# An output projection as one pipeline of 16 token tiles in three stages, with the first up product among its last tiles

## The chip, the cores and the metric

The kernel runs on one core of one Trainium2 chip. The metric is the device time of one execution in microseconds (us); the number given for a kernel is the median of its runs.

## What is computed

One block of a diffusion model on 2048 tokens of 1024 channels. A mixing part makes a vector y of 1024 channels for every token (four branches, not touched here). Then, as the reference has it:

```
mix   = y @ w_out
h     = x + mod2 * rmsnorm(mix, g_post_mix)
hl    = rmsnorm(h, g_pre_ffn) * (1 + mod4) + mod3
f     = conv_ffn(hl, ffn_w_up, ffn_conv_w, ffn_conv_b, ffn_w_down, 32 rows)
out   = h + mod5 * rmsnorm(f, g_post_ffn)
```

conv_ffn multiplies hl by w_up (1024 x 5632), runs a 3x3 convolution over the tokens as a grid of 32 rows of 64, multiplies gelu of one half by the other half, and multiplies by w_down (2816 x 1024).

## The kernel before, in words

Every matrix product is made of three f16 products (high times high, high times low, low times high), with power-of-two scales found on the chip. Tokens are handled in four chunks of 512; a chunk has four tiles of 128 tokens. The kernel is written against a tile framework: each engine's instruction order is settled when the program is built, by program order as the priority and by buffers coming free, and the framework sets the semaphores. A tile with a tag has so many buffers (bufs); the next tile of that tag waits for the oldest to be read out. Memory comes from pools that are opened and closed like a stack; a pool opened on the place of a closed one waits for the closed one's tiles.

**Mixer.** It leaves y in two places: 512 channels in on-chip tiles Y[0] to Y[3] (one per chunk, 8 KB of each partition), the others in DRAM tiles ybc[n].

**Output projection** (lines 833 to 891). The loop runs over the chunks 3, 0, 1, 2. For each chunk it first makes the chunk's scale (lines 834 to 839): a reduction, a tiny product with ones in a PSUM bank of tag C (line 122, the tile "sct"), and some one-column VectorE operations. Then for each of its four tiles:

- Projection. SyncE's queue loads x's rows (xr, line 846, two buffers) and y's DRAM half (yr, line 850, three buffers). VectorE splits y in high and low f16 halves (split, lines 309 and 310, four instructions, tile ysp, three buffers). TensorE runs 48 matmuls of 512 columns into two PSUM banks of tag A, of four (lines 859 to 863).
- Residual (lines 864 to 880). ScalarE squares the two banks with a sum (867), GpSimd takes a power of -1/2 (160), VectorE scales the banks (873), GpSimd adds xr (875), the rows are stored to hlat in DRAM (876), ScalarE squares and sums again (878), GpSimd takes another power (160), VectorE scales into xr (880).
- Channels (lines 881 to 891). TensorE transposes the eight 128x128 blocks into two banks of tag C, of two (885), ScalarE applies scale and shift (888), VectorE makes the high half of hT (890), GpSimd the low half (891). hT, all tokens with channels on the partitions, is what the up products read.

The weights of up product 0 are loaded and split (load_up, lines 812 to 828) ahead of the last chunk, n == 2.

**Feed-forward** (lines 898 to 1076). PSUM's pool ps0 (banks A 4, B 2, C 2) is closed and ps1 (V two of two banks, B 2, C 2) opened; the pool ff is opened on the memory of Y and w_out. 22 products: up(c) (lines 926 to 934) writes z of 128 x 2 x 32 x 64 in eight steps of 24 matmuls (lines 356 to 358) with one eviction each (932); z has two buffers. One loop turn c issues up(c), the weights of up(c + 1) (which take a statistic, whose product with ones is line 122 again, in a bank B of ps1 now; a ScalarE copy 822, another 824, and a GpSimd subtraction 825), the convolution of z of c - 1 on VectorE (lines 938 to 967, 32 instructions of line 956 and two of line 964), and the down products of earlier pairs.

Of the kernel before, what the change touches and what calls it, by code (L numbers as in the profile page):

```python
# [7 lines left out]
F32 = mybir.dt.float32  # L8
F16 = mybir.dt.float16
BF16 = mybir.dt.bfloat16  # L10
I32 = mybir.dt.int32
AF = mybir.ActivationFunctionType
OP = mybir.AluOpType
AX = mybir.AxisListType

D = 1024
L = 2048
LC = 256
CH = 512
NCH = L // CH  # L20
# [48 lines left out]
def block_kernel(ctx: ExitStack, tc: tile.TileContext, x, xT, ctx_d, ctxT, cc, crow, cols_d, wm01, bm01, wmT,  # L69
                 win, wuv, gw, pw, wsT, gnorm, wout, wup, wdn, ident_d, out):  # L70
    nc = tc.nc
    V, A, G, T, S = nc.vector, nc.scalar, nc.gpsimd, nc.tensor, nc.sync
# [4 lines left out]
    small = ctx.enter_context(tc.tile_pool(name="small", bufs=4))  # L77
# [14 lines left out]
    def pA(name):  # L92
        return bank("A", name)

    def pB(name):
        return bank("B", name)

    def pC(name):
        return bank("C", name)
# [3 lines left out]
    hlat = dram.tile([L, D], F32, name="hlat")  # L103
# [52 lines left out]
    def rsqrt(dst, src, n, scale):  # L156

        t = small.tile([128, 12], F32, tag="rst", name="rst")
        V.tensor_scalar(t[:, :n], src, scale, EPS, op0=OP.mult, op1=OP.add)
        G.tensor_tensor(dst, t[:, :n], mhalf[:, :n], op=OP.pow)  # L160

    hT = const.tile([128, 2, KT, L], F16, name="hT")

    wmix = tc.tile_pool(name="ymix", bufs=1)
    ymix = wmix.__enter__()
    Y = [ymix.tile([128, 4, CH], F32, name=f"Y{n}") for n in range(NCH)]
    wsp = tc.tile_pool(name="wsp", bufs=8)
    wspp = wsp.__enter__()
    mixc = tc.tile_pool(name="mix", bufs=1)
# [138 lines left out]
    def split(slot_hi, slot_lo, raw, sc, after=()):  # L308
        hold(V.tensor_scalar(slot_hi, raw, sc[:, 0:1], None, op0=OP.mult), after)
        V.scalar_tensor_tensor(slot_lo, raw, sc[:, 0:1], slot_hi, op0=OP.mult, op1=OP.subtract)  # L310
# [42 lines left out]
    def mm3(ps, wh, wl, hh, hl):  # L353

        for k in range(KT):
            T.matmul(ps, wh(k), hh(k), start=(k == 0), stop=False)  # L356
            T.matmul(ps, wh(k), hl(k), start=False, stop=False)  # L357
            T.matmul(ps, wl(k), hh(k), start=False, stop=(k == KT - 1))  # L358
# [10 lines left out]
    for j in range(4):  # L369
        r = win_raw[j]  # L370
# [308 lines left out]
    wo = {}  # L679
# [150 lines left out]
    gm2 = row_of("gm2", on_, 0, col("gqm", 0, 8))  # L830
    gs_f, sc_f, _ = fold("gsf", col("gpf", 0, 8), mcol[:, 0, 8:16], mcol[:, 0, 16:24])

    for n in (3, 0, 1, 2):
        ysc = small.tile([128, 2], F32, tag="ysc", bufs=2, name="ysc")
        yt = small.tile([128, 1], F32, tag="yt", bufs=2, name="yt")
        V.tensor_reduce(yt, ysq[:, n, :], axis=AX.X, op=OP.add)
        scales(ysc, yt)
        oinv = small.tile([128, 1], F32, tag="oinv", bufs=2, name="oinv")
        V.tensor_scalar(oinv, ysc[:, 1:2], wosc[:, 1:2], None, op0=OP.mult)
        if n == 2:  # L840
            wn, lu = load_up(0)
            list(lu)
        for tt in range(4):
            tok = n * CH + tt * 128
            xr = on_.tile([128, D], F32, tag="xr", name="xr")
            S.dma_start(xr, x[tok:tok + 128, :])
            ysp = op_.tile([128, 2, 8, 128], F16, tag="ysp", bufs=3, name="ysp")
            tw = slice(tt * 128, (tt + 1) * 128)
            yr = op_.tile([128, 4, 128], F32, tag="yr", bufs=3, name="yr")
            S.dma_start(yr, ybc[n][:, :, tw])  # L850
            split(ysp[:, 0, 4:8], ysp[:, 1, 4:8], yr, ysc)
            split(ysp[:, 0, 0:4], ysp[:, 1, 0:4], Y[n][:, :, tw], ysc)
            ps = [pA(f"wo{h}") for h in range(2)]
            order = (6, 7, 4, 5, 0, 1, 2, 3)
            for i, k in enumerate(order):
                wk = wo[k]
                st, sp = i == 0, i == 7
                for h in range(2):
                    T.matmul(ps[h], ysp[:, 0, k, :], wk[:, 0, h * CH:(h + 1) * CH], start=st, stop=False)  # L859
                for h in range(2):  # L860
                    T.matmul(ps[h], ysp[:, 0, k, :], wk[:, 1, h * CH:(h + 1) * CH], start=False, stop=False)  # L861
                for h in range(2):
                    T.matmul(ps[h], ysp[:, 1, k, :], wk[:, 0, h * CH:(h + 1) * CH], start=False, stop=sp)  # L863
            hl = on_.tile([128, D], F32, tag="hl", bufs=2, name="hl")
            ms = small.tile([128, 2], F32, tag="ms", name="ms")
            for h in range(2):
                A.activation(hl[:, h * CH:(h + 1) * CH], ps[h], AF.Square, scale=oinv, accum_out=ms[:, h:h + 1])
            m1 = small.tile([128, 2], F32, tag="m1", name="m1")
            V.tensor_tensor(m1[:, 0:1], ms[:, 0:1], ms[:, 1:2], op=OP.add)
            rsqrt(m1[:, 1:2], m1[:, 0:1], 1, 1.0 / D)  # L870
            V.tensor_scalar(m1[:, 0:1], m1[:, 1:2], oinv, None, op0=OP.mult)
            for h in range(2):
                V.scalar_tensor_tensor(hl[:, h * CH:(h + 1) * CH], ps[h], m1[:, 0:1], gm2[:, h * CH:(h + 1) * CH],
                                       op0=OP.mult, op1=OP.mult)
            G.tensor_tensor(hl, hl, xr, op=OP.add)
            S.dma_start(hlat[tok:tok + 128, :], hl)
            m2 = small.tile([128, 2], F32, tag="m2", name="m2")
            A.activation(xr, hl, AF.Square, accum_out=m2[:, 0:1])
            rsqrt(m2[:, 1:2], m2[:, 0:1], 1, 1.0 / D)
            V.tensor_scalar(xr, hl, m2[:, 1:2], None, op0=OP.mult)  # L880
            h32 = on_.tile([128, 8, 128], F32, tag="h32", bufs=1, name="h32")
            for h in range(2):
                pt = pC("tr")
                for k in range(4):
                    T.transpose(pt[:, k * 128:(k + 1) * 128], xr[:, (4 * h + k) * 128:(4 * h + k + 1) * 128], ident)
                for k in range(4):
                    kk = 4 * h + k
                    A.activation(h32[:, kk, :], pt[:, k * 128:(k + 1) * 128], AF.Identity,  # L888
                                 bias=gs_f[:, 1, kk:kk + 1], scale=gs_f[:, 0, kk:kk + 1])
            V.tensor_scalar(hT[:, 0, :, tok:tok + 128], h32, 1.0, None, op0=OP.mult)  # L890
            G.tensor_tensor(hT[:, 1, :, tok:tok + 128], h32, hT[:, 0, :, tok:tok + 128], op=OP.subtract)

    oc.__exit__(None, None, None)
    wsp.__exit__(None, None, None)
# [1 line left out]


    banks["ffn"] = True
    ff = ctx.enter_context(tc.tile_pool(name="ff", bufs=2))
    oc2.__exit__(None, None, None)  # L900
    fa = ctx.enter_context(tc.tile_pool(name="fa", bufs=2, side="right"))
    close_psum()
    open_psum("ps1", 0, 2, 2)
# [4 lines left out]
    def load_down(gi):  # L908
# [11 lines left out]
        for r, w in zip(rs, ws):  # L920
# [1 line left out]
            A.activation(r, r, AF.Copy, scale=dnsc[:, gi, 0:1])  # L922
            G.tensor_tensor(w[:, 1, :], r, w[:, 0, :], op=OP.subtract)  # L923
            yield

    def up(c, z, w):
        for b in range(4):
            for ab in range(2):
                ps = pB("up")
                mm3(ps, lambda k: w[:, 0, ab, k, :], lambda k: w[:, 1, ab, k, :],  # L930
                    lambda k: hT[:, 0, k, b * CH:(b + 1) * CH], lambda k: hT[:, 1, k, b * CH:(b + 1) * CH])
                A.activation(z[:, ab, b * 8:(b + 1) * 8, :], ps.rearrange("p (r x) -> p r x", x=64),  # L932
                             AF.Identity, scale=upinv[:, c:c + 1])
                yield

    TAPS = [(dy, dx) for dy in (-1, 0, 1) for dx in (-1, 0, 1) if (dy, dx) != (0, 0)]

# [99 lines left out]
    for c in range(NP + 1):  # L1037
        gi, i = divmod(c, GRP)
        if c < NP:
            z = ff.tile([128, 2, 32, 64], F32, tag="z", name="z")  # L1040
            upn, lu = up(c, z, wn), nothing
            if c + 1 < NP:
                wn, lu = load_up(c + 1)
            if i == 0:
                ld = load_down(gi)
        else:
            upn = lu = nothing
        for s in range(8):
            next(upn, None)
            if s > 0:  # L1050
                next(lu, None)
                if s % 2 == 0:
                    next(ld, None)
            if c != NP - 1:
                for _ in range(1 if c < NP else 2):
                    if next(dn, queue) is queue and queue:
                        dn = queue.pop(0)
                        next(dn)
            next(cvn, None)
            if s % 4 == 3 and c > 0 and i == 0:  # L1060
                q = s // 4
                queue.append(down(gi - 1, q, *split_g(gi - 1, q, gs, gsq)))
        if 2 <= c < 10:
            next(mf)
        if c == 10:
            next(mf, None)
            gm5 = row_of("gm5", fa, 3, col("gqf", 0, 8))
        if c < NP:
            if i == 0:
                gs = [[], []]  # L1070
                gsq = small.tile([128, 2, GRP], F32, tag="gsq", bufs=2, name="gsq")
            cvn = conv(c, z, gs, [gsq[:, q, i:i + 1] for q in range(2)])
# [97 lines left out]
```

## Time and profile before

| | |
|---|---|
| median of 3 runs | 2252.57 us (2251.51 to 2254.48) |
| the profiled execution | 2258.45 us, its span 2256.7 us |
| TensorE busy | 2055.7 us, 91% of the span |
| VectorE busy | 1602.1 us, 71% |
| ScalarE busy | 1195.1 us, 53% |
| GpSimd busy | 600.4 us, 27% |
| mean granted clock of TensorE | 0.95 |

The span is the profiled execution from its first instruction to its last, and all stretches below are counted from the span's start. PE is TensorE's matmuls, PEld its weight loads, DVE VectorE, ACT ScalarE, POOL GpSimd, SP SyncE. A matmul's end is modelled, so neighbours overlap in the rows; the distance of two starts is the time that one takes. The granted clock is 1.00 for 2.4 GHz and 0.50 for 1.2 GHz.

### The profile page before, as it was taken

What the parts mean: (1) busy time and instruction counts of PE and PEld (TensorE: products, weight loads), DVE (VectorE), ACT (ScalarE), POOL (GpSimd) and SP (SyncE); (2) the same over time, 40 slices, a digit from 0 to 9 for tenths busy, and PEclk for the clock granted to TensorE, in tenths of its full rate; (3) what the DMA queues carried; (4) which work ended last, traced back from release to release, by engine and by line L of the source; (5) the groups of instructions that cost most, each with busy time, mean ns of one, the idle gap of its engine ahead of it and who ended that gap; (6) DMA issues with size and microseconds to landing.
All of it is one profiled execution on the core that took longest, in us unless ns stands there. A gap on an engine that the chain in (4) does not pass through costs nothing.

```text
span 2256.7 us, 24365 instructions
## 1 busy us (share of the span) xinstructions
PE 2055.7 (91%) x9215; PEld 943.1 (42%) x9215; DVE 1602.1 (71%) x2218; ACT 1195.1 (53%) x1661; POOL 600.4 (27%) x453
## 2 busy tenths in 40 slices
PE   6878989797788779999999999999999999999964
PEld 1533444343334334444444444444444444444421
DVE  6687778999343449977778677867677776777844
ACT  4666755453433355655565554656555564646421
POOL 2332333543333430101122121212121121112144
PEclk8889999898888889999999999999999999999987
DMA  7521143413222221223546454545545454454387
GB/s 284 203 87 51 64 153 122 135 45 125 97 80 80 79 71 37 94 85 123 96 76 130 86 103 88 107 81 100 90 88 108 85 102 72 97 94 84 58 231 252
DMA packets 77514, 239.48 MB, mean 106 GB/s; under 512 B 7890, under 2 KB 18514, under 8 KB 72530
## 3 DMA queue, kind: packets, MB, share of 16 engines
q1 hardware_dynamic: 56660, 162.42, 21.4%
q0 software_dynamic: 20736, 75.51, 20.4%
q8 instruction: 72, 1.18, 0.2%
q14 instruction: 46, 0.38, 0.1%
HBM read 128.84 MB, written 109.05 MB: 105 GB/s over the span
## 4 chain that ended last, share of the span: by engine, by line
PE 57%; issue 4%; DMA 3%; DVE 3%; POOL 2%; ACT 1%; POOLq 0%; SPq 0%; DVEq 0%; ACTq 0%
PE up L356 12%; PE up L357 12%; PE up L358 12%; PE dn L1003 6%; PE dn L1005 6%; PE dn L1004 6%; DVE cv L956 1%; DMA ac<-accd 1%; PE wo L863 1%; PE wo L861 1%; PE wo L859 1%; DMA out_dram<-hr 1%; DMA hr<-hlat 1%; ACT h L888 1%; POOL hr L1027 1%
## 5 line engine op out<-in xcount | busy, mean ns | idle before, releaser
L956 DVE SCALAR_TENSOR_TENSOR cv<-z,cols,cv 128x1008 f32<-128x1008 f32 (+2 forms) x704 | 874.6, 1251 | 290.9 <-ACT cv L949 196.4
L356 PE MATMUL up<-hT,uw 128*128 128x512 f16 x1408 | 534.3, 379 | 4.3 <-ACT h L888 2.2
L357 PE MATMUL up<-hT,uw 128*128 128x512 f16 x1408 | 534.3, 379 | 0.0
L358 PE MATMUL up<-hT,uw 128*128 128x512 f16 x1408 | 534.1, 379 | 0.0
L1018 POOL DMA_DIRECT2D accd<-dd x144 | 124.6, 865 | 763.0 <-ACT dd L1014 756.8
L932 ACT ACTIVATE z<-up,upinv 128x512 f32<-128x512 f32 x176 | 120.8, 686 | 350.8 <-PE up L358 350.2
L1003 PE MATMUL dn<-dw,gs 128*128 128x512 f16 x704 | 271.4, 386 | 35.7 <-DVE ac L1009 32.1
L1014 ACT ACTIVATE dd<-dn,gdi 128x512 f32<-128x512 f32 x320 | 214.2, 681 | 114.0 <-PE dn L1005 107.9
L1004 PE MATMUL dn<-dw,gs 128*128 128x512 f16 x704 | 271.4, 385 | 0.0
L1005 PE MATMUL dn<-dw,gs 128*128 128x512 f16 x704 | 269.4, 385 | 0.0
L357 PEld LDWEIGHTS <-uw 128*128 128x128 f16 x1408 | 137.8, 98 | 169.2 <-issue 5.0
L356 PEld LDWEIGHTS <-uw 128*128 128x128 f16 x1408 | 139.0, 99 | 165.2 <-issue 0.8
L358 PEld LDWEIGHTS <-uw 128*128 128x128 f16 x1408 | 137.9, 98 | 166.6 <-issue 0.8
L825 POOL TENSOR_TENSOR uw<-ur,uw 128x2048 f16<-128x2048 f32 x22 | 89.5, 4068 | 201.2 <-ACT ur L824 201.2
L136 ACT ACT_TABLE_LOAD x77 | 98.8, 1283 | 48.2 <-PE rp L440 29.9
L1004 PEld LDWEIGHTS <-gs 128*128 128x128 f16 x704 | 69.6, 99 | 119.5 <-issue 44.8
L949 ACT ACTIVATE cv<-z,cols 128x1024 f32<-128x1024 f32 x88 | 106.1, 1205 | 2.3
L1003 PEld LDWEIGHTS <-gs 128*128 128x128 f16 x704 | 73.0, 104 | 81.2 <-issue 5.1
L1005 PEld LDWEIGHTS <-gs 128*128 128x128 f16 x704 | 69.8, 99 | 86.2 <-issue 5.5
L859 PE MATMUL wo<-wo,ysp 128*128 128x512 f16 x256 | 81.3, 401 | 10.0 <-ACT gm L804 7.8
L863 PE MATMUL wo<-wo,ysp 128*128 128x512 f16 x256 | 77.4, 387 | 4.9 <-DVE ysp L310 4.9
L923 POOL TENSOR_TENSOR dw<-dr,dw 128x1024 f16<-128x1024 f32 x22 | 46.4, 2124 | 129.8 <-PE dn L1005 100.6
(299 smaller groups left out, 3042.8 us busy)
## 6 DMA issues: line engine op xcount, KB each, us to landing
accd<-dd POOLq DMA_DIRECT2D x144, 512.0 KB, 5.4
ur<-in_wup_dram SPq DMA_DIRECT2D x22, 1024.0 KB, 5.6
wm<-in_wmT_dram SPq DMA_DIRECT2D x64, 256.0 KB, 2.9
dr<-in_wdn_dram SPq DMA_DIRECT2D x22, 512.0 KB, 4.1
hT<-in_wm_dram SPq DMA_DIRECT2D x8, 1024.0 KB, 14.6
xt<-in_xT_dram SPq DMA_DIRECT2D x8, 1024.0 KB, 7.3
ro<-in_wout_dram SPq DMA_DIRECT2D x16, 512.0 KB, 3.6
xr<-in_x_dram SPq DMA_DIRECT2D x16, 512.0 KB, 4.1
```

Of the source, the lines that this page charges most:

```text
L356: T.matmul(ps, wh(k), hh(k), start=(k == 0), stop=False)
L357: T.matmul(ps, wh(k), hl(k), start=False, stop=False)
L358: T.matmul(ps, wl(k), hh(k), start=False, stop=(k == KT - 1))
L859: T.matmul(ps[h], ysp[:, 0, k, :], wk[:, 0, h * CH:(h + 1) * CH], start=st, stop=False)
L932: A.activation(z[:, ab, b * 8:(b + 1) * 8, :], ps.rearrange("p (r x) -> p r x", x=64), AF.Identity, scale=upinv[:, c:c + 1])
L949: A.activation(t, z[:, ab, r0:r0 + 16, :].rearrange("p r x -> p (r x)"), AF.Identity, bias=col("fcb", c + NP * ab), scale=wt(0, 0))
L956: V.scalar_tensor_tensor(o, z[:, ab, ya + dy:yb + dy, xa + dx:xb + dx], wt(dy, dx), o, op0=OP.mult, op1=OP.add)
L1003: T.matmul(ps[h], hi, wh, start=i == 0, stop=False)
L1004: T.matmul(ps[h], hi, wl, start=False, stop=False)
L1005: T.matmul(ps[h], lo, wh, start=False, stop=i == n - 1)
L1014: A.activation(d[:, h * CH:(h + 1) * CH], ps[h], AF.Copy, scale=di)
L1018: G.dma_start(accd[t], d, accum_op=OP.add)
```

## The change

The chunk loop becomes one loop of 18 turns over 16 tiles, in the chunk order 3, 2, 1, 0. Turn i issues the projection of tile i, the residual of tile i - 1 and the channels of tile i - 2, in this order. The bodies of the three stages are the old lines. The scales of the first two chunks are made ahead of the loop, those of the others two tiles after the start of the chunk two places earlier, that is six tiles ahead. xr has three buffers instead of two. up moves ahead of the loop and takes an order of blocks; up(0) is issued with the blocks 3, 2, 1, 0, two steps in each of the turns 16 and 17 and the other four after the loop. Its z has the memory of Y[2] and Y[3], in a new pool zp that stays open; z of the even c lies in zp, of the odd c in ff. The pool outn is closed ahead of the opening of ff. The weights of up(0) are issued in turn 5.

```diff
+    zp = ctx.enter_context(tc.tile_pool(name="zp", bufs=1))
-    Y = [ymix.tile([128, 4, CH], F32, name=f"Y{n}") for n in range(NCH)]
+    Y23 = zp.tile([128, 2, 32, 64], F32, tag="z", name="Y23")
+    Y = [ymix.tile([128, 4, CH], F32, name=f"Y{n}") for n in range(2)]
+    Y += [Y23[:, e].rearrange("p r x -> p (r x)").rearrange("p (j t) -> p j t", j=4) for e in range(2)]
...
-    for n in (3, 0, 1, 2):
-        ysc = small.tile([128, 2], F32, tag="ysc", bufs=2, name="ysc")
+    def up(c, z, w, order=(0, 1, 2, 3)):
+        for b in order:
...
+    def y_scale(n):
+        ysc = small.tile([128, 2], F32, tag="ysc", bufs=4, name="ysc")
...
+    def project(n, tt):
...
+        xr = on_.tile([128, D], F32, tag="xr", bufs=3, name="xr")
...
+    def residual(n, tt, ps, xr):
...
+    def channels(n, tt, xr):
...
+    OUT = (3, 2, 1, 0)
+    tiles = [(n, tt) for n in OUT for tt in range(4)]
+    y_scale(OUT[0])
+    y_scale(OUT[1])
+    z0, up0 = None, None
+    pr = {}
+    for i in range(len(tiles) + 2):
+        if i < len(tiles):
+            n, tt = tiles[i]
+            if tt == 2 and OUT.index(n) + 2 < NCH:
+                y_scale(OUT[OUT.index(n) + 2])
+            pr[i] = project(n, tt)
+        if i == 5:
             wn, lu = load_up(0)
             list(lu)
...
+        if 0 <= i - 1 < len(tiles):
+            residual(*tiles[i - 1], *pr[i - 1])
+        if i == len(tiles):
+            z0 = zp.tile([128, 2, 32, 64], F32, tag="z", name="z")
+            up0 = up(0, z0, wn, OUT)
+        if up0 is not None:
+            next(up0)
+            next(up0)
+        if i >= 2:
+            channels(*tiles[i - 2], pr.pop(i - 2)[1])
+    for _ in up0:
+        pass
...
     banks["ffn"] = True
+    oc2.__exit__(None, None, None)
     ff = ctx.enter_context(tc.tile_pool(name="ff", bufs=2))
-    oc2.__exit__(None, None, None)
...
-            z = ff.tile([128, 2, 32, 64], F32, tag="z", name="z")
-            upn, lu = up(c, z, wn), nothing
+            z = (ff if c % 2 else zp).tile([128, 2, 32, 64], F32, tag="z", bufs=1, name="z") if c else z0
+            upn, lu = up(c, z, wn) if c else nothing, nothing
```

## Rows read from the trace of the kernel before

**Rows 1.** Page, busy time of the engines: us, share of span, instructions.
```profile
PE 2055.7 (91%) x9215; PEld 943.1 (42%) x9215; DVE 1602.1 (71%) x2218; ACT 1195.1 (53%) x1661; POOL 600.4 (27%) x453
```

**Rows 2.** Windows: four chunks, up(0), up(1), the rest; columns as headed.
```profile
core 0: us, PE busy (x) PEld busy (x) DVE busy (x) ACT busy (x) POOL busy (x), PEclk, DMA share, GB/s
558.80:619.90 61.10, 49.48 (x227) 24.04 (x228) 23.78 (x56) 24.11 (x59) 20.04 (x15) 0.86 0.35 119
619.90:684.00 64.10, 50.59 (x226) 24.13 (x226) 26.25 (x53) 21.78 (x56) 22.33 (x16) 0.85 0.25 82
684.00:748.00 64.00, 50.96 (x229) 24.78 (x230) 26.26 (x53) 21.78 (x56) 22.31 (x16) 0.87 0.25 85
748.00:809.80 61.80, 48.02 (x224) 23.17 (x223) 24.88 (x54) 29.52 (x64) 26.40 (x17) 0.89 0.26 90
809.80:854.30 44.50, 43.79 (x197) 19.80 (x197) 25.10 (x28) 18.65 (x19) 10.42 (x4) 0.96 0.16 54
854.30:896.00 41.70, 41.39 (x194) 18.99 (x193) 40.79 (x40) 20.48 (x22) 4.08 (x1) 1.00 0.07 26
1000.00:2150.00 1150.00, 1146.48 (x5374) 527.27 (x5373) 846.66 (x894) 649.25 (x811) 229.34 (x177) 1.00 0.48 93
```

**Rows 3.** Timeline of TensorE, end of the third chunk: start, us, instruction, idle before.
```profile
734.34 1.06 PE L885 MATMUL tr<-ident,xr 128*128 128x128 f32 x8 [1.76 <-DVE m L869]
743.44 1.94 PE L885 MATMUL tr<-ident,xr 128*128 128x128 f32 x8 [8.03 <-DVE xr L880]
746.19 0.59 PE L122 MATMUL sct<-yt,ones 128*128 128x1 f32 x2 [0.81 <-ACT h L888]
752.63 0.60 PE L863 MATMUL wo<-wo,ysp 128*128 128x512 f16 x2 [1.25 <-DVE ysp L310]
```

**Rows 4.** Waits of TensorE from 558.7 to 854.3: us, times, longest.
```profile
PE tr L885 <- DVE xr L880: 33.0, 4, 8.6
PE up L356 <- ACT h L888: 2.2, 1, 2.2
```

**Rows 5.** Chain of waits inside a chunk: start, us, what.
```profile
714.43 0.43 PE wo L861 x2
714.87 0.87 PE tr L885 x8
715.74 0.43 PE wo L863 x2
```

**Rows 6.** Windows: the first 5.1 us, then one tile inside a chunk.
```profile
558.80:563.90 5.10, 5.10 (x13) 1.75 (x14) 5.10 (x14) 0.33 (x1) 0.00 (x0) 0.50 0.98 355
714.70:726.37 11.67, 11.67 (x60) 5.80 (x58) 3.54 (x8) 5.39 (x14) 5.96 (x5) 1.00 0.25 91
```

**Rows 7.** Timelines of the engines, turn from the projection to up(0).
```profile
809.82 0.59 PE L356 MATMUL up<-hT,uw 128*128 128x512 f16 x1 [2.20 <-ACT h L888]
...
816.87 0.69 ACT L932 ACTIVATE z<-up,upinv 128x512 f32<-128x512 f32 x1 [7.10 <-PE up L358]
821.99 0.69 ACT L932 ACTIVATE z<-up,upinv 128x512 f32<-128x512 f32 x1 [4.43 <-PE up L358]
...
821.79 0.28 PE L122 MATMUL sct<-stt,ones 128*128 128x1 f32 x2
...
822.57 1.99 ACT L822 ACTIVATE uw<-ur,upsc 128x2048 f16<-128x2048 f32 x1
...
826.68 4.08 POOL L825 TENSOR_TENSOR uw<-ur,uw 128x2048 f16<-128x2048 f32 x1 [13.98 <-ACT ur L824]
828.47 1.21 ACT L949 ACTIVATE cv<-z,cols 128x1024 f32<-128x1024 f32 x1
```

**Rows 8.** Timeline of SyncE's queue, third chunk.
```profile
689.24 13.52 SPq L850 DMA_DIRECT2D yr<-ybc  x4
708.13 0.34 SPq L876 DMA_DIRECT2D hlat<-hl  x1
715.77 0.33 SPq L846 DMA_DIRECT2D xr<-in_x_dram  x1
```

**Rows 9.** Timeline of GpSimd and VectorE around 749.5.
```profile
749.34 2.30 POOL L891 TENSOR_TENSOR hT<-h,hT 128x1024 f16<-128x1024 f32 x1 [6.83 <-DVE hT L890]
...
749.69 2.22 DVE L309 TENSOR_SCALAR ysp<-yr,ysc 128x512 f16<-128x512 f32 x1
```

**Rows 10.** Groups by shape: busy, mean ns; idle before and its enders.
```profile
L875 POOL TENSOR_TENSOR hl<-hl,xr 128x1024 f32<-128x1024 f32 x16 | 37.6, 2348 | 29.7 <-DVE hl L873 29.7
...
L964 DVE TENSOR_TENSOR g<-g,cv 128x1024 f32<-128x1024 f32 x44 | 53.7, 1220 | 2.4 <-ACT z L932 0.4
```

**Rows 11.** Page, costliest group; DMA view, median us from issue to landing.
```profile
L956 DVE SCALAR_TENSOR_TENSOR cv<-z,cols,cv 128x1008 f32<-128x1008 f32 (+2 forms) x704 | 874.6, 1251 | 290.9 <-ACT cv L949 196.4
...
yr<-ybc SPq DMA_DIRECT2D x16, 256.0 KB, 3.3
```

More of the change, by code (lines that the diff above doesn't have):

```diff
@@ L831, in block_kernel @@
     gs_f, sc_f, _ = fold("gsf", col("gpf", 0, 8), mcol[:, 0, 8:16], mcol[:, 0, 16:24])
-    for n in (3, 0, 1, 2):
-        ysc = small.tile([128, 2], F32, tag="ysc", bufs=2, name="ysc")
+    def up(c, z, w, order=(0, 1, 2, 3)):
+        for b in order:
+            for ab in range(2):
+                ps = pB("up")
+                mm3(ps, lambda k: w[:, 0, ab, k, :], lambda k: w[:, 1, ab, k, :],
+                    lambda k: hT[:, 0, k, b * CH:(b + 1) * CH], lambda k: hT[:, 1, k, b * CH:(b + 1) * CH])
+                A.activation(z[:, ab, b * 8:(b + 1) * 8, :], ps.rearrange("p (r x) -> p r x", x=64),
+                             AF.Identity, scale=upinv[:, c:c + 1])
+                yield
+    yscale = {}
+    def y_scale(n):
+        ysc = small.tile([128, 2], F32, tag="ysc", bufs=4, name="ysc")
         yt = small.tile([128, 1], F32, tag="yt", bufs=2, name="yt")
@@ L837, in block_kernel @@
         scales(ysc, yt)
-        oinv = small.tile([128, 1], F32, tag="oinv", bufs=2, name="oinv")
+        oinv = small.tile([128, 1], F32, tag="oinv", bufs=4, name="oinv")
         V.tensor_scalar(oinv, ysc[:, 1:2], wosc[:, 1:2], None, op0=OP.mult)
-        if n == 2:
+        yscale[n] = ysc, oinv
+    def project(n, tt):
+        tok = n * CH + tt * 128
+        ysc = yscale[n][0]
+        xr = on_.tile([128, D], F32, tag="xr", bufs=3, name="xr")
+        S.dma_start(xr, x[tok:tok + 128, :])
+        ysp = op_.tile([128, 2, 8, 128], F16, tag="ysp", bufs=3, name="ysp")
+        tw = slice(tt * 128, (tt + 1) * 128)
+        yr = op_.tile([128, 4, 128], F32, tag="yr", bufs=3, name="yr")
+        S.dma_start(yr, ybc[n][:, :, tw])
+        split(ysp[:, 0, 4:8], ysp[:, 1, 4:8], yr, ysc)
+        split(ysp[:, 0, 0:4], ysp[:, 1, 0:4], Y[n][:, :, tw], ysc)
+        ps = [pA(f"wo{h}") for h in range(2)]
+        for i, k in enumerate((6, 7, 4, 5, 0, 1, 2, 3)):
+            wk = wo[k]
+            st, sp = i == 0, i == 7
+            for h in range(2):
+                T.matmul(ps[h], ysp[:, 0, k, :], wk[:, 0, h * CH:(h + 1) * CH], start=st, stop=False)
+            for h in range(2):
+                T.matmul(ps[h], ysp[:, 0, k, :], wk[:, 1, h * CH:(h + 1) * CH], start=False, stop=False)
+            for h in range(2):
+                T.matmul(ps[h], ysp[:, 1, k, :], wk[:, 0, h * CH:(h + 1) * CH], start=False, stop=sp)
+        return ps, xr
@@ new lines, in residual @@
+    def residual(n, tt, ps, xr):
+        tok = n * CH + tt * 128
+        oinv = yscale[n][1]
+        hl = on_.tile([128, D], F32, tag="hl", bufs=2, name="hl")
+        ms = small.tile([128, 2], F32, tag="ms", name="ms")
+        for h in range(2):
+            A.activation(hl[:, h * CH:(h + 1) * CH], ps[h], AF.Square, scale=oinv, accum_out=ms[:, h:h + 1])
+        m1 = small.tile([128, 2], F32, tag="m1", name="m1")
+        V.tensor_tensor(m1[:, 0:1], ms[:, 0:1], ms[:, 1:2], op=OP.add)
+        rsqrt(m1[:, 1:2], m1[:, 0:1], 1, 1.0 / D)
+        V.tensor_scalar(m1[:, 0:1], m1[:, 1:2], oinv, None, op0=OP.mult)
+        for h in range(2):
+            V.scalar_tensor_tensor(hl[:, h * CH:(h + 1) * CH], ps[h], m1[:, 0:1], gm2[:, h * CH:(h + 1) * CH],
+                                   op0=OP.mult, op1=OP.mult)
+        G.tensor_tensor(hl, hl, xr, op=OP.add)
+        S.dma_start(hlat[tok:tok + 128, :], hl)
+        m2 = small.tile([128, 2], F32, tag="m2", name="m2")
+        A.activation(xr, hl, AF.Square, accum_out=m2[:, 0:1])
+        rsqrt(m2[:, 1:2], m2[:, 0:1], 1, 1.0 / D)
+        V.tensor_scalar(xr, hl, m2[:, 1:2], None, op0=OP.mult)
@@ new lines, in channels @@
+    def channels(n, tt, xr):
+        tok = n * CH + tt * 128
+        h32 = on_.tile([128, 8, 128], F32, tag="h32", bufs=1, name="h32")
+        for h in range(2):
+            pt = pC("tr")
+            for k in range(4):
+                T.transpose(pt[:, k * 128:(k + 1) * 128], xr[:, (4 * h + k) * 128:(4 * h + k + 1) * 128], ident)
+            for k in range(4):
+                kk = 4 * h + k
+                A.activation(h32[:, kk, :], pt[:, k * 128:(k + 1) * 128], AF.Identity,
+                             bias=gs_f[:, 1, kk:kk + 1], scale=gs_f[:, 0, kk:kk + 1])
+        V.tensor_scalar(hT[:, 0, :, tok:tok + 128], h32, 1.0, None, op0=OP.mult)
+        G.tensor_tensor(hT[:, 1, :, tok:tok + 128], h32, hT[:, 0, :, tok:tok + 128], op=OP.subtract)
@@ L841, in block_kernel @@
+    OUT = (3, 2, 1, 0)
[11 more added lines that the diff above has]
+        if i == 5:
             wn, lu = load_up(0)
             list(lu)
[L843 to L891, printed above, removed]
@@ L924, in load_down @@
             yield
[L926 to L934, printed above, removed]
     TAPS = [(dy, dx) for dy in (-1, 0, 1) for dx in (-1, 0, 1) if (dy, dx) != (0, 0)]
```

## The prediction

> **What bounds the kernel now.** I read the page first, then the windows by stage, then TensorE's timeline and waits where a window shows idle time. On the page TensorE is busy for 91% of the span, the other engines far less [rows 1]. The share hides two regimes. From 1000 to 2150 TensorE is busy for 1146.48 of 1150 us at a granted clock of 1.00 (2.4 GHz) [rows 2]: the feed-forward part is bound by it, and what starts earlier there ends earlier. The four chunks of the output projection take 61.1, 64.1, 64.0 and 61.8 us with TensorE busy for 48 to 51 of each, at a mean clock of 0.85 to 0.89 [rows 2].
>
> The timeline at the end of a chunk shows why [rows 3]. The last tile's transposes wait 8.03 us for its residual, the next chunk's scale product (sct) stands behind them on TensorE and waits for the eviction that frees its bank, the splits wait for the scale, the matmuls for the splits. The chunk's scale is the gate: nothing of the next chunk can be projected before it. The wait for xr comes four times, 33.0 us in all [rows 4], and the fourth is ahead of up(0), whose first block needs only tokens done long before; it waits for the last eviction (2.2 us [rows 4]), that is, for PSUM's pool to change hands. Inside a chunk nothing of this is seen: matmuls start 0.43 us a pair, eight transposes take 0.87 [rows 5], and TensorE is busy throughout [rows 6].
>
> So the stretch to shorten runs from the first output matmul, 558.8, to the first of up(1), 854.3: 295.5 us. Its floor is matmul time at full clock.
>
> **The change, part by part**, as the time of that stretch after.
>
> *Sixteen tiles without drains.* Scales made six tiles ahead take the gate away; the residual of one tile has a whole turn to run in, the transposes another. A tile costs TensorE 24 pairs x 0.43 + 0.87 = 11.2 us [rows 5], sixteen 179.0. The window of one tile shows 11.67, but with a pair more than a tile has (60 instructions where 56 are one tile's [rows 6]); as an upper end it gives 16 x 0.48 = 7.7 us more. Can the others keep the pace? In that window VectorE was busy for 3.54, ScalarE for 5.39, GpSimd for 5.96 us [rows 6]. The splits, which fell outside it, add to VectorE, so I take the mean of a chunk: 26.25 / 4 = 6.6 [rows 2]. All stay well under 11.2.
>
> *The start* stays: the first 5.1 us run at 0.50 (1.2 GHz) with 13 matmuls [rows 6], about 2.5 us lost. The four scale products remain, now between matmuls: 0.59 each at most [rows 3], mostly overlapped; I take 1 us together.
>
> *up(0) among the last tiles.* Its 192 matmuls cost 96 x 0.43 = 41.3 us wherever they stand. Two steps (10.3 us) cover the last residual and two more the transposes' turn, so the last drain costs nothing; block 0, which needs the last tile, comes behind another 10.3 us of block 1. If this cover failed, one drain of some 10 us would come back. z in the memory of Y[2] and Y[3] waits for splits finished eight tiles earlier: nothing. The weights of up(0), issued in turn 5, cost ScalarE and GpSimd about 4 us each, once, beside matmuls: nothing.
>
> *What loses its cover.* up(1) needs weights whose statistic uses a bank of the new PSUM pool, and that pool waits for the old one, now for up(0)'s last eviction. Before, this chain ran beside up(0): sct at 821.79, the copies from 822.57, the subtraction finished at 826.68 + 4.08 = 830.76 [rows 7], 9.0 us. After, nothing is left for TensorE to do beside it: the eviction 0.69, the chain 9.0, and half of one convolution instruction of 1.21 in ScalarE's way [rows 7], 10.4 us. It is bounded by 0 below (if the statistic were let in earlier) and above by 16 (both convolution instructions in the way, 1.8 more, and another GpSimd operation as long as the 4.08 ahead of the subtraction). I take 10.4: the rows show these same instructions. Behind an idle stretch of that kind the first up step took from 809.82 to 816.87, the second 5.12 [rows 7], at 0.96 mean clock in the stretch [rows 2]: 1.9 us more.
>
> *Queues.* The loads and stores are the same in number. xr's third buffer lets a load wait for the transposes two turns on. The down weights now load behind the last channels, under two up steps: nothing. What waits in SyncE's queue is a rival below. Pool order and buffer counts of the scales: nothing.
>
> Sum: 179.0 + 2.5 + 1.0 + 41.3 + 10.4 + 1.9 = 236.1, that is 59.4 us less than 295.5. The profiled execution would go from 2258.45 to 2199.0; it stands 5.9 above the median of 2252.57, so the median goes to **2193**. From the two open terms the likeliest case reaches from 2187 to 2201.
>
> **The rivals.**
>
> *The end chain is hidden after all.* If the build let the statistic's product in before up(0) ends, 10.4 + 1.9 us fall away. The convolution of product 0 then shows: VectorE needs 874.6 / 22 + 2 x 1.22 = 42.2 us for it [rows 10, 11], up(1) 41.3, and up(2) waits for that z: 2 us back. About 2183. Against it: up(0) itself waited for the pool [rows 4].
>
> *VectorE and GpSimd hold each other up.* A split that takes about half a microsecond alone took 2.22 us when it began 0.35 us behind a GpSimd subtraction of 2.30, and ended only as that one had [rows 9]. GpSimd's per tile are 5.6 us (22.31 / 4 [rows 2]), 2.35 of them in one addition [rows 10]. If VectorE stood still for all of them, a tile would need 6.6 + 5.6 = 12.2 us against 11.2, and the sum grows by 16 x 1.0 = 16 us: 2209. For it: the stages now overlap fully. Against it: chunk means of VectorE already hold such waits, and not every operation does so. The Trainium skill says of this, in "SBUF — State Buffer", section "SBUF: two separate sides", that the two engines share a pair of ports under an exclusive lock, held for a whole instruction. By that rule the rival's price is full; these rows agree for this pair of instructions.
>
> *The lead of the convolution is lost.* Before, it began at 828.47 [rows 7], 25.8 us ahead of up(1). After, up(0) ends with block 0, which the first convolution reads, so it begins with the end chain. If TensorE came to wait for it, up to 25.8 us return: 2219. Against it: up(2) can start no sooner than 10.4 + 1.9 + 41.3 = 53.6 us after up(0), and the convolution is done by 44.
>
> *Slower: SyncE's queue.* The next tile's xr waits for a buffer until the transposes two tiles back, which now come at the end of a turn. If yr stands behind it in the queue, the projection waits each turn for the issue 0.33 [rows 8], the landing 3.3 [rows 11] and the first split, about 1 us: 4.6 x 15 = 69 us, giving 2262, and up to 15 x 2.5 more where the clock falls as at the start. It decides above 59.4 / 15 = 4.0 us a turn. Against it: the order before sends four yr loads in a row ahead of the stores and of xr [rows 8], as their buffers come free sooner.
>
> *The change does nothing:* the builder's order brings the gate back in another place, 2252.
>
> **How the numbers follow.** The likeliest case 0.55; the hidden chain 0.12; the held engines 0.15; the lost lead 0.08; the queue 0.05; nothing 0.03; 0.02 for others. From 2181 to 2219 is left out about 0.15 to 0.2. 0.2% is 4.5 us, about what can be told from no change. Faster: the first four and a little, 0.91; same 0.03; slower 0.06.
>
> **What would show it.** Right: TensorE's waits for xr gone, a clock of 1.00 from the sixth microsecond of the stage to the end of up(0), tiles 11.2 us apart, then one hole of about 10 us with a statistic's product at its head, then TensorE full again. Wrong: holes between tiles, ended by splits (then ask whether a DMA, VectorE or the scale was late); transposes waiting for xr; no hole ahead of up(1); or holes around up(2), ended by an eviction or the convolution.

## The result, and the profile after

The changed kernel takes 2198.95 us (median of 4 runs, 2195.05 to 2199.91), the kernel before, beside it on the same chip, 2253.36 (4 runs): a ratio of 0.9756, 95% interval 0.9739 to 0.9773. Forecast were 2193 in 2181 to 2219. The profiled execution took 2195.05 us, span 2193.3.

The page of the changed kernel, busy time of the engines (us, share of the span, instructions), as in [rows 1]:

```profile
PE 2034.2 (93%) x9215; PEld 935.4 (43%) x9215; DVE 1593.0 (73%) x2218; ACT 1192.5 (54%) x1661; POOL 603.0 (27%) x453
```

The number of instructions is the same, and TensorE is busy for 21.5 us less: matmuls that ran at 1.2 GHz now run at 2.4. The windows of the changed kernel: the projection's start, the rest up to up(0)'s last eviction, one tile in it, up(1), and the feed-forward part. The columns are those of [rows 2]; the last three are clock, DMA share, GB/s.

```profile
553.10:558.20 5.10, 5.08 (x16) 1.91 (x17) 5.10 (x18) 0.00 (x0) 0.00 (x0) 0.63 0.92 349
558.20:777.30 219.10, 218.39 (x1078) 107.33 (x1076) 90.06 (x193) 101.38 (x242) 97.80 (x65) 1.00 0.29 100
642.50:653.73 11.23, 11.23 (x57) 5.61 (x56) 5.47 (x12) 5.62 (x15) 6.17 (x5) 1.00 0.35 121
777.30:835.20 57.90, 47.20 (x203) 20.80 (x204) 56.16 (x59) 30.40 (x32) 12.30 (x4) 0.85 0.17 55
983.40:2088.00 1104.60, 1101.68 (x5164) 506.30 (x5163) 817.13 (x865) 623.28 (x781) 224.79 (x176) 1.00 0.50 94
```

The half-idle chunks of [rows 2] are gone: TensorE is busy for 218.39 of 219.10 us at 2.4 GHz, through all sixteen tiles and up(0). Then comes a stretch that was full before and isn't now: up(1), busy for 47.20 of 57.90 us at 0.85, where [rows 2] had 41.39 of 41.70 at 1.00. TensorE's waits from 553 to 840 (us, times, longest) name what it waits for:

```profile
PE up L361 <- POOL uw L828: 6.3, 1, 6.3
PE up L359 <- ACT uw L825: 3.7, 1, 3.7
PE wo L874 <- ACT gm L807: 1.1, 1, 1.1
PE sct L122 <- ACT z L842: 0.8, 1, 0.8
PE up L359 <- ACT z L842: 0.7, 1, 0.7
```

No wait for xr is left of the 33.0 us of [rows 4]. The large ones are for up(1)'s weights: the high half (L825) and the low half (L828).

To compare kernels I cut each profile at four rows: the first output matmul, the end of up(0)'s last eviction, the end of up(1)'s last, and the end of the last up eviction. A stretch is one such time less the one before, in us of the profiled execution.

| kernel | median us | ratio to before, interval | output and up(0) | up(1) | up(2) to up(21) |
|---|---|---|---|---|---|
| before | 2253.36 | | 296.2 | 42.0 | 1224.8 |
| changed | 2198.95 | 0.9756 (0.9739 to 0.9773) | 224.2 | 57.9 | 1225.1 |
| scales alone | 2198.72 | 0.9757 (0.9744 to 0.9770) | 244.4 | 42.0 | 1224.1 |
| pipeline alone | 2204.12 | 0.9781 (0.9768 to 0.9794) | 246.5 | 42.0 | 1224.9 |
| gate back | 2222.69 | 0.9853 (0.9835 to 0.9870) | 244.8 | 57.6 | 1225.8 |
| two tiles ahead | 2197.86 | 0.9761 (0.9744 to 0.9778) | 224.5 | 57.9 | 1225.5 |
| two xr | 2199.14 | 0.9764 (0.9751 to 0.9778) | 224.5 | 56.5 | 1225.9 |
| copies first | 2199.02 | 0.9762 (0.9748 to 0.9776) | 224.5 | 53.8 | 1228.0 |
| low products last | 2191.14 | 0.9723 (0.9707 to 0.9739) | 224.7 | 51.8 | 1225.5 |
| kept warm | 2196.95 | 0.9749 (0.9732 to 0.9766) | 224.5 | 58.4 | 1225.3 |
| statistic early | 2189.07 | 0.9709 (0.9694 to 0.9724) | 224.4 | 43.8 | 1228.5 |
| the same, lower rows first | 2187.56 | 0.9708 (0.9692 to 0.9724) | 224.7 | 43.8 | 1227.4 |
| the same, starter first | 2190.60 | 0.9723 (0.9701 to 0.9744) | 225.2 | 43.8 | 1232.6 |

So the stage gave 72.0 us, up(1) took back 15.8, net 56.2; the medians differ by 54.4. The profiled executions differ by 63.4, because the first output matmul came 5.7 us sooner, the tail (from the last up eviction to the span's end) was 1.9 us shorter, and up(2) to up(21) took 0.3 us more. The last experiment is about the 5.7 and the 1.9.

### The profile page after: what moved, and what is told of

Same layout as the page of the kernel before. It is cut to its first block, busy times and chain, and to the rows that moved or that the text cites. A ratio compares the mean times of both kernels' runs of the same rounds, so it can differ in the third digit from the quotient of the medians.

```text
span 2193.3 us, 24364 instructions
## 1 busy us (share of the span) xinstructions
PE 2034.2 (93%) x9215; PEld 935.4 (43%) x9215; DVE 1593.0 (73%) x2218; ACT 1192.5 (54%) x1661; POOL 603.0 (27%) x453
## 4 chain that ended last, share of the span: by engine, by line
PE 69%; DVE 13%; DMA 6%; issue 5%; ACT 5%; POOL 2%; SPq 0%; POOLq 0%; DVEq 0%; ACTq 0%
PE up L359 13%; PE up L361 13%; PE up L360 13%; PE dn L1049 6%; PE dn L1051 6%; PE dn L1050 6%; PE wo L874 3%; PE wo L876 3%; PE wo L878 3%; DVE wm L660 2%; DMA ac<-accd 1%; DMA wm<-in_wmT_dram 1%; DVE lru L479 1%; ACT L136 1%; DMA hT<-in_wm_dram 1%
## 5 line engine op out<-in xcount | busy, mean ns | idle before, releaser
L828 POOL TENSOR_TENSOR uw<-ur,uw 128x2048 f16<-128x2048 f32 x22 | 89.5, 4068 | 196.8 <-ACT ur L827 165.2
```

## The experiments

**Which part brings the gain.** The kernel before with nothing but the four scales made ahead of its chunk loop (buffers 2 to 4), and the changed kernel with up(0) back in the first turn of the feed-forward loop:

```diff
+    yscale = {}
     for n in (3, 0, 1, 2):
-        ysc = small.tile([128, 2], F32, tag="ysc", bufs=2, name="ysc")
+        ysc = small.tile([128, 2], F32, tag="ysc", bufs=4, name="ysc")
...
+        yscale[n] = ysc, oinv
+
+    for n in (3, 0, 1, 2):
+        ysc, oinv = yscale[n]
```

> The kernel before with only the four chunk scales made ahead of the chunk loop; sequential tile bodies, two xr buffers, order 3, 0, 1, 2. My theory: the chunk scale was the gate, and the order builder pipelines the tiles by itself once it is gone, as inside a chunk; three drains of 17 to 19 us go (61.1 + 64.1 + 64.0 - 12 x 11.2 - 2.5 = 52 us), the last one stays: about 2201 us. Rival, that the three stages in the program's order are what makes the tiles overlap: half of that or less, 2225 us or more.

```diff
-            up0 = up(0, z0, wn, OUT)
...
-            upn, lu = up(c, z, wn) if c else nothing, nothing
+            upn, lu = up(c, z, wn), nothing
```

> The changed kernel with up(0) put back into the first turn of the feed-forward loop (blocks 0, 1, 2, 3; z still in the memory of Y[2] and Y[3]). My theory: the overlap of up(0) with the last tiles brings nearly nothing, since the drain that it covers (61.8 - 4 x 11.2 = 17 us in the kernel before) comes back, and in exchange the preparation of up(1)'s weights, 15.8 us of the second product in the changed kernel, is again covered by up(0). So about 2200 us, within 4 us of the changed kernel's 2199. Rival, that the placement of up(0) is an essential part of the gain: the drain comes back and nothing is returned, 2215 us or more.

The scales alone give 2198.72, the whole change's time. The old loop, with the gate gone, pipelines by itself: the builder's order lets a later tile's matmuls pass the earlier one's transposes. Only the last drain is left, as the first row of TensorE's waits from 553 to 840 shows for the kernel with the scales alone:

```profile
PE tr L890 <- DVE xr L885: 12.2, 2, 11.4
```

The same waits from 553 to 803, of the kernel with the pipeline alone:

```profile
PE tr L910 <- ACT h L913: 8.8, 4, 5.9
...
PE up L359 <- DVE hT L915: 5.5, 1, 5.5
```

The pipeline alone has that drain too: 246.5 against 224.2, 22.3 us for 16.1 us of idle time and the lower clock behind it. That is what up(0) among the last tiles covers. But the 15.8 us exposed ahead of up(1) go against it: 6.2 by the profiles, 5.2 by the medians. So the moved product is worth 5 to 6 us here (the two intervals just overlap), a little more than the 4 that I had allowed. The loop in three stages shows no gain by itself: the pipeline alone is no faster than the scales alone (2204.12 against 2198.72), and neither is the whole change.

**Is it the gate, and how far ahead must it go?** The changed kernel with each scale made at the start of its own chunk, and with each made two tiles ahead instead of six:

```diff
-    y_scale(OUT[0])
-    y_scale(OUT[1])
...
-            if tt == 2 and OUT.index(n) + 2 < NCH:
-                y_scale(OUT[OUT.index(n) + 2])
+            if tt == 0:
+                y_scale(n)
```

> The changed kernel with each chunk's scale made at the start of its own chunk again, all else as changed. If being made behind the last transposes of the chunk before was the harm, then here, where the transposes of only the tile three turns back stand ahead of it, little comes back: 2199 to 2206 us. Rival, that the distance of six tiles is needed: a hole of 17 us at each of three chunk starts, 2240 us or more.

```diff
-    y_scale(OUT[1])
...
-            if tt == 2 and OUT.index(n) + 2 < NCH:
-                y_scale(OUT[OUT.index(n) + 2])
+            if tt == 2 and OUT.index(n) + 1 < NCH:
+                y_scale(OUT[OUT.index(n) + 1])
```

> The changed kernel with each chunk's scale product made two tiles ahead (inside the chunk before) instead of six. My theory: what mattered was that the scale doesn't stand behind the last transposes of the chunk before, so two tiles (22 us of PE's work) are enough: 2199, within 4, PE idle 0 in the stretch to the end of up(0). Rival (the lead has to be long, since the splits of the activations are held by GpSimd and queue behind the residuals on VectorE): some of the 24 us come back that the product at the chunk's own start cost, 2207 to 2223, with PE waiting on the activations' splits at each chunk's start.

The gate comes back and costs 23.7 us by the medians, a miss of my 2199 to 2206 and of the rival's 2240. This kernel keeps the four buffers of the scales, so it is their place and not the buffers that counts. Two tiles ahead cost nothing, so the distance of six is more than is needed. The kernel with the gate back, timeline at the second chunk's start (start, us, instruction, idle before):

```profile
606.00 0.38 PE L122 MATMUL sct<-yt,ones 128*128 128x1 f32 x2 [1.89 <-ACT h L913]
...
607.38 2.88 POOL L896 TENSOR_TENSOR hl<-hl,xr 128x1024 f32<-128x1024 f32 x1 [1.83 <-DVE scq L127]
...
608.16 2.39 DVE L312 TENSOR_SCALAR ysp<-yr,ysc 128x512 f16<-128x512 f32 x1
...
610.22 2.31 POOL L916 TENSOR_TENSOR hT<-h,hT 128x1024 f16<-128x1024 f32 x1
...
610.59 2.22 DVE L312 TENSOR_SCALAR ysp<-Y,ysc 128x512 f16<-128x512 f32 x1
```

The scale product stands behind a tile's transposes again, and two of the splits that follow take 2.39 and 2.22 us where 0.47 is usual; each begins beside a GpSimd instruction (2.88, 2.31) and ends 0.3 us behind its end. The hole of the second chunk's start has 5.0 us of idle time. At the third and fourth TensorE does not idle at all: the builder fills these holes with steps of up(0), the first at 658.9. That is why the price isn't 40. But then up(0) is used up when the last drain comes, and TensorE waits there, for 6.9 us in all:

```profile
PE up L359 <- DVE hT L915: 5.7, 1, 5.7
```

**The third xr buffer.**

```diff
-        xr = on_.tile([128, D], F32, tag="xr", bufs=3, name="xr")
+        xr = on_.tile([128, D], F32, tag="xr", bufs=2, name="xr")
```

> The changed kernel with two residual buffers of 128x1024 instead of three, everything else as it is. A tile's residual then waits for the residual of the tile before the last to be stored and its two halves transposed. In the trace of the changed kernel tile i's residual is loaded while tile i-1's is being normalized, and tile starts lie 11.23 us apart at PE without a gap. My theory: the three-stage pipeline holds at most two residuals between their load and their transposes for all but a few us of a tile, so this costs nothing: 2199, within 4. Rival (the third buffer is what the pipeline needs): every tile loses the time between the load and the reading of the residual, 2 us or more on each of 16 tiles, 2230 or above, and PE shows a wait for xr or for DVE's residual in every tile.

2199.14, no difference; TensorE has no idle time in the sixteen tiles there either. The third buffer can go, and SyncE's queue holds nobody up.

**Who sets the hole ahead of up(1).** The changed kernel, its hole (start, us, instruction, idle before), which answers to [rows 7]:

```profile
776.62 0.69 ACT L842 ACTIVATE z<-up,upinv 128x512 f32<-128x512 f32 x1 [4.49 <-PE up L361]
777.35 2.34 ACT L995 ACTIVATE cv<-z,cols 128x1024 f32<-128x1024 f32 x2
777.37 0.60 PE L122 MATMUL sct<-stt,ones 128*128 128x1 f32 x4 [0.78 <-ACT z L842]
779.62 1.99 ACT L825 ACTIVATE uw<-ur,upsc 128x2048 f16<-128x2048 f32 x1
781.51 2.17 ACT L977 ACTIVATE dw<-dr,dnsc 128x1024 f16<-128x1024 f32 x2
781.66 0.61 PE L359 MATMUL up<-hT,uw 128*128 128x512 f16 x1 [3.69 <-ACT uw L825]
783.59 1.99 ACT L827 ACTIVATE ur<-ur,upsc 128x2048 f32<-128x2048 f32 x1
785.71 4.07 POOL L828 TENSOR_TENSOR uw<-ur,uw 128x2048 f16<-128x2048 f32 x1 [24.27 <-ACT ur L827]
789.83 0.61 PE L361 MATMUL up<-hT,uw 128*128 128x512 f16 x1 [6.28 <-POOL uw L828]
```

ScalarE does both of the convolution's starters (2.34) ahead of the first copy, and two copies of the down weights (2.17) between the first copy and the second. Put behind:

```diff
+            second[c] = A.activation(r, r, AF.Copy, scale=upsc[:, c, 0:1])
...
-            A.activation(w[:, 0, :], r, AF.Copy, scale=dnsc[:, gi, 0:1])
+            hold(A.activation(w[:, 0, :], r, AF.Copy, scale=dnsc[:, gi, 0:1]), [second[1]] if gi == 0 else ())
...
-                A.activation(t, z[:, ab, r0:r0 + 16, :].rearrange("p r x -> p (r x)"), AF.Identity,
-                             bias=col("fcb", c + NP * ab), scale=wt(0, 0))
+                hold(A.activation(t, z[:, ab, r0:r0 + 16, :].rearrange("p r x -> p (r x)"), AF.Identity,
+                                  bias=col("fcb", c + NP * ab), scale=wt(0, 0)), [second[1]] if c == 0 else ())
```

> The changed kernel with ScalarE's two convolution starters (2.34 us together) and its two copies of the down weights (2.17 us) put behind the two copies of up(1)'s weights instead of ahead of and between them. My theory of the term that was mis-sized: these stood ahead of the needed copies in ScalarE's order. The first copy begins some 1.4 us sooner, the second 3.6 sooner, so up(1)'s stretch falls from 57.85 to 54 us and the time to 2195, within 2.5. Rival (GpSimd's splits of 4.07 us each, or the clock, set the stretch): no change, 2199 within 2; or the starters that now come later hold up the convolution by as much as is gained, which would show as a stretch from up(1)'s end to the last up product that is 3 to 4 us longer.

up(1)'s stretch falls by 4.0, as the first theory had it; the stretch behind it grows by 2.9, and the time stays at 2199.02, close to what the second rival had (3 to 4 longer). The convolution began at 786.09, 7.2 us after the eviction instead of 1.3, and TensorE then waits for its product (the kernel with the copies first, from 832 to 890):

```profile
PE sct L122 <- DVE gt L1020: 2.0, 1, 2.0
```

The hole can be shortened without touching ScalarE's order. TensorE did four matmuls in it and then met one with the low half. So here up(1)'s first two steps do all products with the high half of the weights first:

```diff
+        for k in range(KT):
+            T.matmul(ps, wh(k), hh(k), start=(k == 0), stop=False)
+            T.matmul(ps, wh(k), hl(k), start=False, stop=False)
+        for k in range(KT):
+            T.matmul(ps, wl(k), hh(k), start=False, stop=(k == KT - 1))
...
-                mm3(ps, lambda k: w[:, 0, ab, k, :], lambda k: w[:, 1, ab, k, :],
+                (mm_late if c == 1 and b == 0 else mm3)(ps, lambda k: w[:, 0, ab, k, :], lambda k: w[:, 1, ab, k, :],
```

> The changed kernel, where up(1)'s first two steps do all products with the high half of the weights first (32 matmuls) and those with the low half (16) last; the same products are summed in another order. In the changed kernel TensorE did four matmuls in the hole and then waited 6.3 us for the low half. My theory of the hole: its second part is only the order of the products, so these 32 matmuls cover it. The wait for GpSimd's subtraction goes, the wait of 3.7 us for the first copy stays, and the clock comes back sooner: up(1)'s stretch 48 to 51 us instead of 57.85. As the run with the copies first showed, part comes back as the convolution's lost lead, 2 to 4 us: the time 2192 to 2197. Rival: all of it comes back, 2199 within 2.

2191.14, just under the 2192 to 2197 expected, and hardly anything is given back (1225.5 against 1225.1): the rival falls, and so does my own 2 to 4 us of lost lead. Its largest waits of TensorE from 770 to 835:

```profile
PE up L358 <- ACT uw L832: 3.7, 1, 3.7
PE sct L122 <- ACT uw L151: 2.2, 1, 2.2
```

Its windows of the hole and behind it:

```profile
779.00:786.00 7.00, 2.53 (x10) 1.10 (x9) 5.48 (x12) 6.61 (x6) 0.00 (x0) 0.71 0.00 0
786.00:792.00 6.00, 6.00 (x23) 2.48 (x22) 6.00 (x6) 4.39 (x4) 3.56 (x1) 0.77 0.00 0
792.00:824.00 32.00, 29.62 (x138) 13.38 (x137) 31.13 (x31) 16.32 (x17) 8.78 (x4) 1.00 0.28 100
```

The wait of 6.3 is gone. The stretch is 51.8 instead of the expected 48 to 51, because a statistic's product now waits 2.2 us in it.

**The clock by itself.** Forty matmuls that nothing reads, in the hole:

```diff
             next(upn, None)
+            if c == 1 and s == 0:
+                warm = pC("warm")
+                for _ in range(40):
+                    T.matmul(warm, hT[:, 0, 0, 0:128], hT[:, 0, 1, 0:CH], start=True, stop=True)
```

> The changed kernel with 40 matmuls of 512 columns that compute nothing needed, into a PSUM bank that is free, in the hole ahead of up(1) (36 behind the statistic's product, 4 behind the first two up matmuls). At 2.4 GHz they fill about 8.6 of the hole's 12 us; the copies and the subtraction, which the needed matmuls wait for, are on other engines and stay as they are. My theory of the clock: of the 15.8 us by which up(1)'s stretch grew, 11.1 are idle time and 4.7 the lower clock at both sides of it, a consequence of the idle time. With the filling the granted clock stays 1.00, the first needed low-half matmul still starts some 12.5 us after the last eviction, and the stretch falls to 53 to 54 us; the time 2194 to 2199, since part comes back as lost lead. Rival: the lower clock has nothing to do with the idle time, or the filling delays the needed matmuls: a stretch of 58 us or more, 2199 or above.

Its windows through the hole and behind it:

```profile
782.00:790.00 8.00, 8.00 (x39) 3.64 (x39) 8.00 (x14) 8.00 (x7) 0.10 (x1) 1.00 0.01 2
790.00:796.00 6.00, 3.63 (x18) 1.49 (x16) 6.00 (x6) 1.85 (x2) 6.00 (x2) 1.00 0.13 25
...
804.00:808.00 4.00, 1.73 (x7) 0.69 (x7) 3.96 (x5) 2.22 (x4) 0.00 (x0) 0.89 0.00 0
808.00:812.00 4.00, 4.00 (x14) 1.56 (x13) 4.00 (x6) 2.00 (x1) 0.00 (x0) 0.68 0.00 0
```

The changed kernel's windows, beside the first two of these:

```profile
781.00:790.00 9.00, 2.05 (x5) 0.56 (x6) 9.00 (x9) 6.66 (x6) 4.29 (x2) 0.50 0.00 0
790.00:796.00 6.00, 6.00 (x15) 2.06 (x14) 6.00 (x7) 1.40 (x1) 3.94 (x2) 0.52 0.86 274
```

The lower clock did come from the idle time: filled, the hole and what follows up to 804 run at 1.00. But the stretch is 58.4, not 53 to 54, and the time shows no gain: 2196.95, with an interval that overlaps that of the changed kernel. ScalarE and TensorE in the kept-warm kernel:

```profile
803.37 1.06 ACT L151 ACTIVATE junk<-g 128x1024 bf16<-128x1024 f32 x1
...
804.42 1.19 ACT L995 ACTIVATE cv<-z,cols 128x1024 f32<-128x1024 f32 x1
805.55 0.67 ACT L842 ACTIVATE z<-up,upinv 128x512 f32<-128x512 f32 x1
...
806.27 0.38 PE L359 MATMUL up<-hT,uw 128*128 128x512 f16 x1 [2.44 <-ACT z L842]
```

TensorE has done its first 48 needed matmuls 22.3 us after up(0)'s last eviction instead of 25.2. The third step then waits for the eviction of the second, and this stands behind other work in ScalarE's order; the step starts only 1.1 us sooner than in the changed kernel, 24.8 us after the eviction instead of 25.9. In this new wait of 2.4 us the clock fell, and that cost more than the 1.1 us. The clock theory holds, the stretch was a miss.

**The chain let in early.** Raw weights and statistic of up(1) in turn 9, while the old PSUM pool is open:

```diff
+        if i == 9:
+            early[1] = raw_up(1)
...
+            scale_up(1, junk.bitcast(BF16).rearrange("p (a m) -> p a m", a=2), early[1])
```

> The changed kernel with one thing moved: the raw weights of up(1) are loaded and their statistic is made in turn 9 of the pipeline, with its product in a bank of the old PSUM pool, so that only two copies and a subtraction are left, which need no PSUM. My theory: the hole ahead of up(1) (idle 0.8, 3.7 and 6.3 us, and a clock of 0.50 behind it) is that statistic waiting for up(0)'s last eviction; it closes to about 1 us, and 12 to 15 us of the 15.8 are gained, less some 2 to 3 us that up(2) then waits for the first convolution: about 2187 us. Rival, that the hole is the memory of the pool ff coming free late, or the convolution: the hole stays, 2197 to 2201 us.

The best so far, 9.9 us under the changed kernel. Its copies and the subtraction now lie ahead of up(0)'s end (the kernel with the statistic early, around 765):

```profile
762.47 1.99 ACT L835 ACTIVATE uw<-ur,upsc 128x2048 f16<-128x2048 f32 x1
764.50 2.00 ACT L837 ACTIVATE ur<-ur,upsc 128x2048 f32<-128x2048 f32 x1
...
766.63 4.08 POOL L838 TENSOR_TENSOR uw<-ur,uw 128x2048 f16<-128x2048 f32 x1 [4.39 <-ACT ur L837]
```

up(1) shrinks by 14.1 and 3.4 come back behind it, at a wait for the gate's product. From 821 to 1010:

```profile
PE sct L122 <- DVE gt L1032: 3.2, 1, 3.2
```

Two attempts to win these back, the halves of the first convolution in the other order, and its starter ahead of a square of up(2)'s weights:

```diff
-        for q in range(2):
+        for q in ((1, 0) if c == 0 else (0, 1)):
```

> The kernel with up(1)'s raw weights and statistic in turn 9 (2189.1, measured), and the convolution of product 0 begins with the lower half of the rows instead of the upper. That kernel showed 7.6 us of idle PE in the first turns of the convolution, 3.2 of it for the gate product's operand, where the changed kernel has 4.4 in all. My theory: those 3.4 us are the lead of the convolution that up(1) without a hole no longer gives, and the order of the halves decides when the first half's work can begin (its rows are there when up(0) ends, whichever half; the neighbours' rows of the second half come free sooner): 2184 to 2187. Rival (both halves of z are complete when the convolution begins, so the order moves nothing): 2189, within 2.

```diff
+        hold(A.activation(junk, src, AF.Square, scale=SQ, accum_out=dst), start)
...
+                if c == 0 and q == 0:
+                    start.append(s)
```

> The kernel with up(1)'s raw weights and statistic in turn 9 (2189.1, measured), where the square of up(2)'s weights is put behind the convolution's first starter on ScalarE. In that kernel this square (1.90 and 0.19 us) stood ahead of the starter: the convolution began 3.0 us after the last eviction of up(0), in the changed kernel 1.3 us after it, and from the end of up(1) to the last up product 1228.5 us went by instead of 1225.1. My theory: up(1) without a hole leaves the convolution no slack, so that what it begins late comes back as TensorE's waits in the next turns. With the starter first it begins some 2 us sooner, and the stretch after up(1) falls to 1226 to 1227: the time 2186 to 2188. Rival: VectorE's own rate in the first turns sets it, whatever the start: 1228.5 and 2189 again, within 1.5.

The first gives 2187.56; its interval covers that of the kernel it starts from, so no gain is shown. The second is a miss: the convolution did begin 1.3 us after the eviction, but the wait grew from 3.2 to 4.7 and the stretch to 1232.6. That the convolution's start sets what comes back is not what this run shows. VectorE is busy for 53.45 of the 54.0 us from 826 here and for 52.47 of the 54.0 from 824 in the kernel that it starts from, which fits the rival, VectorE's own rate, though not its 1228.5; which of VectorE's instructions decides stays open.

**The kernel before, once more.**

> The kernel before, unchanged, for another profile of it. The first output matmul started at 558.8 in its profile and between 553.1 and 556.7 in those of the kernels with the scales ahead of the loop, although the mixer's instructions are the same. If this is how executions differ, it starts anywhere from 552 to 559 here; if the change moved it, at 558 to 559 again. From the first output matmul to the end of up(1) it should take 338 us, within 1, either way.

First output matmul at 557.5, then 338.8 us to the end of up(1), and a tail of 133.0 us as the changed kernel has it (134.8 in the first profile). So the tail's 1.9 us are no part of the change. The eleven kernels with scales ahead of their chunks start between 553.1 and 557.0, the kernel with the gate back at 558.5. In the first two profiles TensorE has the same 1859 instructions ahead of the second scale product, and 5.6 of the 5.7 us are there by the 700th, deep in the mixer. So none of the 5.7 is shown to be the change's; with one profile each it can't be excluded either.

## Why the prediction was right, and where it was off

*The gate*: right. Removing it alone brings all that the change brings, putting it back costs 23.7 us. What the rest of the change adds to that the prediction did not ask: what the covered drain gives, the exposed chain mostly takes.

*The stage's sum*: 179.0 + 2.5 + 1.0 + 41.3 = 223.8 were forecast up to the end of up(0)'s matmuls. Measured: 776.6 - 553.1 = 223.5. A tile takes 11.23 (forecast 11.2), the clock is 1.00 from 558.2 on, the sixth microsecond. The start was milder, 0.63 instead of 0.50.

*The cover of the last drain*: it does cover it, but "one drain of some 10 us" was too small: 22.3, as the pipeline alone shows.

*The end chain*: the term that was mis-sized. I took 10.4 us with "half of one convolution instruction" in ScalarE's way. From the last eviction's start to the low half's first matmul it was 789.83 - 776.62 = 13.2, inside the bound of 16: the statistic's product came 2.25 us ahead of the first copy instead of 0.78, and two copies of the down weights stood ahead of the second, where nothing had stood. The starters are in [rows 7]; the copies of the down weights are in no row (before they ran from 839.74, behind the chain), and the prediction put the down weights at nothing under "Queues". That all of these would come free at the same moment, and in this order, I did not ask.

*The clock*: 1.9 forecast. Behind the hole, 6.0 us at 0.52 lose 6.0 x 0.48 = 2.9. Together with 12.5 us from the eviction's end to the low half's first matmul, and 0.7 since up(1) had begun that much ahead of the eviction's end before, less 0.9 for the four matmuls done in the hole, this accounts for 15.2 of the 15.8 us; 12.3 had been forecast. So the gain was 56.2 by the profiles where 59.4 were forecast, and 54.4 by the medians.

*The rivals.* The hidden chain did not come by itself, but the experiment that let it in gave 2189, with 3.4 us back where the rival counted 2. VectorE is held beside GpSimd in single instructions (2.39 us above), yet no tile is longer for it: in the changed kernel one of the 32 splits of this kind took 2.35 us, the others 0.47 to 0.49, and VectorE is busy for 5.47 of 11.23 us in a tile. The Trainium skill, "SBUF — State Buffer", section "SBUF: two separate sides", gives the two engines a shared pair of ports under a lock held for a whole instruction, for VectorE's part only in a two-port mode or with two inputs from SBUF. The split of 2.39 us beside the addition of 2.88 agrees. The rival's full price does not come out: it had VectorE stand still for all of GpSimd's time. The convolution's lost lead cost next to nothing in the changed kernel (1225.1 against 1224.8). With the hole gone 3.4 us come back, with the low products last 0.3; that the 3.4 are the lost lead is not shown, since an earlier start did not win them back. SyncE's queue cost nothing.

## What to carry to other kernels

A loop that idles at the seams between its parts may need only the one small product that every part waits for: move that first and let the builder pipeline, before the loop is rewritten. When work is moved into another stage's hole, look up what ran beside it where it stood, and list everything that comes free at the same event on each engine in its order, as that list is the exposed chain. If a chain is exposed, see whether its first part can be made ahead of the hand-over (2189.07 here), or let TensorE first do the products that need only the chain's early part (2191.14).

## What was not expected of the hardware

The clock can follow small holes as well. With the large hole filled, TensorE idled only from about 803.9 to 806.27, for 2.4 us, after another such wait ahead of 794.04; the granted clock was 0.89 in the window from 804 and 0.68 in the next, 1.2 GHz for a part of each, although TensorE was at work again in between. Not every such hole does it: the kernel with the low products last waited for 2.2 us up to 799.26, and its window from 792 to 824 shows 1.00. The kernel with the statistic early, with 1.5 us of idle time in up(1), shows 1.00 throughout. What sets these holes apart stays open.
